# Attention steps every 14 groups, operand sums parked in memory, weight sums made one product earlier

## The chip, the cores and the metric

The kernel runs on one core of one Trainium2 chip. The metric is the device time of one execution in microseconds. A profile of one execution goes with it: TensorE (PE, with its weight loads PEld), VectorE (DVE), ScalarE (ACT), GpSimd (POOL, idle here) and SyncE (SP), on whose queue all transfers are issued.

## What is computed

One step of one decoder layer, for a new sequence of 1024 positions and eight sample streams of eight new tokens each, all in float32:

```
proj = einsum('bld,de->ble', x, w_in)          # 1088 rows, 2048 -> 10752
gb, gc, h, z_c, q, k, v, z_a, gate_c, gate_a = split(proj)
y_c = silu(z_c) * gb * short_conv(gc * h)
o   = window attention with sinks and ALiBi (prompt: blocks of 128; samples: 128 cached keys + 8 new)
y_a = silu(z_a) * o
merged = sigmoid(gate_c) * (y_c @ w_conv_out) + sigmoid(gate_a) * (y_a @ w_attn_out)
y = layer_norm(ALPHA * x + merged @ w_out)
```

The updated key and value windows and convolution states are returned too. For the sample streams, all but eight rows of each new window are the old cache, copied.

## The kernel before, in words

**Units and products.** Each large matrix product is cut into units: one unit makes 2 x 128 output columns for all 1088 rows over half of the inner dimension, by one level of the Strassen-Winograd scheme, with seven products instead of eight. Each product is four groups of six matmuls (each operand is split into a high and a low part of a reduced-precision type, and three of the four cross products are kept). A unit is thus 28 groups. Stage a does all 42 units (a0 to a41) with the first half of the inner dimension and stores the partial results (`pd<-ca`); stage b does them again with the second half (b0 to b41, in another order: keys and values, queries, gates, convolution), adding to what was stored (`cb<-pd`); stage m merges (m0_0 to m0_7 over the convolution's half, m1_0 to m1_7 over the attention's); a last stage multiplies by w_out and normalises. In the profile the accumulators of the units are `psa37a`, `psb0c`, `psm_0b` and so on. The three letters name three accumulators of one unit. Four of the seven products go into the first (a), so what a product left there has to be taken out (`take`, an addition into `ca`, `cb` or `cm`) before the product after the next one may start.

**Weights.** The weights of a unit (`wra`, `wrb`, `wrm`, 1 MB) are loaded during the unit before it. For products 2, 3 and 6 sums of weight blocks are needed, four DVE instructions per unit (into `wsa`/`wsb`/`wsm` or in place). Then ACT casts the high part and DVE subtracts to get the low part. `run` issues this three products ahead; the sums stand directly ahead of the cast that reads them, in `Unit.high`.

**Operands.** The other operand is the same for all units of a stage: seven sets of four tiles, resident in SBUF. When a stage's last unit ends, the next stage's set i replaces the old set i as soon as its product i is through (`Operands.put`): per tile a cast on ACT and a subtraction on DVE. Four of the seven sets are sums of loaded blocks, 16 DVE subtractions or additions in all: eight (`combine`) are made ahead, the eight for sets 4 and 5 (`t1` and `p4`) stand between the casts. `load_all` (called by `ahead_of`) issues 16 loads in one go.

**Attention and samples.** Everything else is put between the groups. `agenda` lists work by group number, and `tick` runs after each group: it does what is due, and one entry (`pieces`) of `line`, the operands' queue. An attention step is one head pair times one block of 128 rows, 64 steps in all, one every `STEP` groups, starting in unit b3; the table in `Step.__init__` says how many groups after the step's start each piece of it is issued. `sample` does the same for one of eight pieces of the sample attention, one per gate unit. All small accumulators (`sc`, `pt`, `po`, `sps`, `spo`) share two PSUM banks, `ax`, in turn: a third may only be written when all readers of the first are done.

**Order.** Every engine executes in the order in which the program issues (`InOrder` ties each instruction to the one before it on its engine), transfers on SP included. So one instruction that waits holds up everything behind it on its engine.

## Time and profile before

| | |
|---|---|
| time, median of 3 runs | 2726.74 us (2724.79 to 2728.77) |
| the profiled execution's own time | 2725.17 us |
| its span, first to last instruction | 2723.1 us |
| mean granted TensorE clock | 0.990 |
| PE busy | 2639.6 us, 97% of the span |
| DVE busy | 1757.8 us, 65% |
| ACT busy | 1057.7 us, 39% |
| transfers | 415.97 MB, 45.4% of 16 engines' span |

Busy time of PE is not peak rate: when the granted clock (PEclk) halves, matmuls take longer and count as busier. The length of a unit is therefore the plainer measure: a unit with no wait lasts 21.09 us (a36, a40, b23, b24 and all others of stage a but the first and a37), plus 1.3 us for each attention step within it and 2.1 us for a sample piece.

### The profile page before, as it was taken

What the parts mean: (1) busy time and instruction counts of PE and PEld (TensorE: products, weight loads), DVE (VectorE), ACT (ScalarE), POOL (GpSimd) and SP (SyncE); (2) the same over time, 40 slices, a digit from 0 to 9 for tenths busy, and PEclk for the clock granted to TensorE, in tenths of its full rate; (3) what the DMA queues carried; (4) which work ended last, traced back from release to release, by engine and by line L of the source; (5) the groups of instructions that cost most, each with busy time, mean ns of one, the idle gap of its engine ahead of it and who ended that gap; (6) DMA issues with size and microseconds to landing.
All of it is one profiled execution on the core that took longest, in us unless ns stands there. A gap on an engine that the chain in (4) does not pass through costs nothing. (4 is left out here: it accounts for less than half of the span.)

```text
span 2723.1 us, 47823 instructions
## 1 busy us (share of the span) xinstructions
PE 2639.6 (97%) x19426; PEld 2545.0 (93%) x19426; DVE 1757.8 (65%) x3371; ACT 1057.7 (39%) x2074; POOL 0.2 (0%) x4
## 2 busy tenths in 40 slices
PE   8999999999999999989989999999999999899998
PEld 7999999999999999989989999999999999788886
DVE  7444444444444878868878898888766867533836
ACT  4232332323222535555554545454432433322221
POOL 0000000000000000000000000000000000000000
PEclk9999999999999999999999999999999999999999
DMA  4322232223333366665545545455546565733543
GB/s 160 114 96 97 103 120 98 97 96 115 110 137 121 141 211 205 202 201 168 152 164 162 176 138 155 152 171 170 187 170 216 185 233 195 254 99 110 183 144 102
DMA packets 167327, 415.97 MB, mean 153 GB/s; under 512 B 23442, under 2 KB 75666, under 8 KB 139172
## 3 DMA queue, kind: packets, MB, share of 16 engines
q1 hardware_dynamic: 167108, 412.92, 45.4%
q8 instruction: 153, 2.51, 0.4%
q14 instruction: 66, 0.54, 0.1%
HBM read 295.33 MB, written 119.48 MB: 152 GB/s over the span
## 5 line engine op out<-in xcount | busy, mean ns | idle before, releaser
L97 PE MATMUL o<-wo,m 128*128 128x512 f32 x1344 | 320.6, 394 | 0.2 <-DVE r L1166 0.2
L97 PEld LDWEIGHTS o<-wo,m 128*128 128x128 f32 x1344 | 254.5, 189 | 55.7 <-issue 0.6
L97 DVE TENSOR_TENSOR wa<-wra,wa 128x512 fp32r<-128x512 f32 x210 | 144.5, 689 | 221.6 <-ACT wa L97 221.6
L97 ACT CAST wb<-wrb 128x512 fp32r<-128x512 f32 x210 | 127.3, 616 | 141.4 <-DVE wrb L97 129.3
L1088 DVE TENSOR_TENSOR wo<-wraw,wo 128x512 fp32r<-128x512 f32 x112 | 76.6, 686 | 148.9 <-ACT wo L1087 148.8
L97 DVE TENSOR_TENSOR wb<-wrb,wb 128x512 fp32r<-128x512 f32 x210 | 143.7, 684 | 42.1 <-ACT wb L97 40.4
L1087 ACT CAST wo<-wraw 128x512 fp32r<-128x512 f32 x112 | 69.3, 621 | 220.2 <-PE o L97 193.2
L97 ACT CAST wa<-wsa 128x512 fp32r<-128x512 f32 x84 | 52.1, 621 | 256.4 <-DVE wsa L97 256.4
L97 ACT CAST wa<-wra 128x512 fp32r<-128x512 f32 x210 | 126.3, 622 | 43.2 <-DVE wra L97 33.1
L97 DVE TENSOR_TENSOR wa<-wsa,wa 128x512 fp32r<-128x512 f32 x84 | 58.0, 692 | 93.2 <-ACT wa L97 93.1
L97 ACT CAST wb<-wsb 128x512 fp32r<-128x512 f32 x84 | 51.6, 614 | 152.6 <-DVE wsb L97 150.7
L97 ACT ACTIVATE p<-p,nm 128x256 f32<-128x256 f32 (+1 forms) x128 | 62.5, 489 | 88.7 <-DVE nm L97 88.5
L97 DVE TENSOR_TENSOR wm<-wrm,wm 128x512 fp32r<-128x512 f32 x80 | 55.1, 689 | 46.4 <-ACT wm L97 43.3
L97 ACT ACTIVATE p<-p,den 128x256 f32<-128x256 f32 (+1 forms) x128 | 56.5, 489 | 64.6 <-DVE den L97 63.1
L97 DVE TENSOR_TENSOR wb<-wsb,wb 128x512 fp32r<-128x512 f32 x84 | 57.7, 687 | 35.6 <-ACT wb L97 35.4
L97 ACT ACT_TABLE_LOAD x58 | 74.4, 1283 | 1.7 <-PEq L1331 0.7
L97 ACT CAST wm<-wsm 128x512 fp32r<-128x512 f32 x32 | 19.9, 621 | 107.9 <-DVE wsm L97 107.9
L97 ACT CAST wm<-wrm 128x512 fp32r<-128x512 f32 x80 | 48.4, 621 | 32.2 <-DVE wrm L97 30.5
L97 PEld LDWEIGHTS first<-xa,wa 128*128 128x128 f32 x336 | 46.7, 205 | 12.7 <-ACT wa L97 5.6
L97 PE MATMUL first<-xa,wa 128*128 128x272 f32 x336 | 48.1, 308 | 9.9 <-ACT wa L97 4.0
L97 DVE TENSOR_TENSOR o<-po,ot 64x128 f32<-64x128 f32 x128 | 35.9, 280 | 27.1 <-ACT ot L97 26.0
L97 DVE TENSOR_TENSOR pp<-pt,pp 128x512 fp32r<-128x512 f32 (+1 forms) x64 | 41.7, 651 | 12.9 <-ACT pp L97 12.8
(1072 smaller groups left out, 6507.3 us busy)
## 6 DMA issues: line engine op xcount, KB each, us to landing
pd<-ca SPq DMA_DIRECT2D x42, 1088.0 KB
cb<-pd SPq DMA_DIRECT2D x42, 1088.0 KB
wra<-in_win SPq DMA_DIRECT2D x42, 1024.0 KB
wrb<-in_win SPq DMA_DIRECT2D x42, 1024.0 KB
wraw<-in_wo SPq DMA_DIRECT2D x128, 256.0 KB
sgd<-cb SPq DMA_DIRECT2D x16, 1088.0 KB
sg<-sgd SPq DMA_DIRECT2D x64, 272.0 KB
qt<-qd SPq DMA_DIRECT2D x128, 128.0 KB
```

What stands on the lines that cost most here:

```text
L97: first = f(*args, **kw)
L1087: nc.scalar.copy(hi, raw)
L1088: nc.vector.tensor_sub(lo, raw, hi.bitcast(F32))
```

## The change

Six things change, and no matmul, DVE or ACT instruction is added or removed.

- `STEP` goes from 15 to 14 groups, so that a unit of 28 groups holds exactly two attention steps, and each step's pieces fall at the same places of every unit. The table of places is moved by up to two groups. The table of `sample` is stretched from 38 to 59 groups. The two sigmoids of a gate unit are now issued one directly after the other. One gate unit (`gate_unit(9)`) is moved ahead of the convolution's units, the two others between them are moved, and `open_merge` starts in `gate_unit(12)` instead of 13.
- The copies of the old caches (`copies`, two transfers of 960 KB within device memory) are issued at the start of unit a4 instead of with the samples, and the 16 small stores of new rows are spread, one every 5 groups.
- The weight sums get a function of their own (`Unit.sums`), issued at the end of each product for a product that is one further ahead than the cast.
- `Operands.begin` replaces `ahead_of` and `load_all` for x1 and for both halves of the merge: four loads every 7 or 8 groups; 44 or 50 groups after its start it makes all 16 sums, one after each group, and stores the sums for sets 4 and 5 (`t1`, `p4`) in device memory; it then loads two blocks again.
- `Operands.put` fetches `t1` and `p4` back instead of computing them.
- With this come 24 transfers more for each of the three operand sets, 72 in all.

```diff
-STEP = 15
+STEP = 14
...
+        def begin(self, gap, wait):
+            self.kept = {n: [dram(f"x{n}{self.name}{k}", [P, HALF]) for k in range(4)] for n in ("t1", "p4")}
...
+            for i, what in enumerate(((0, 1, "b"), (1, 1, "c"), (0, 0, "a"), (1, 0, "d"))):
+                after(1 + gap * i, lambda what=what: part(*what))
+            def sums():
+                t3, t2, t1, p4 = (parts[t] for t in "bacd")
+                for op, out, x, y in (
+                    (ve.tensor_sub, t3, t1, t3), (ve.tensor_add, t2, t3, t2),
+                    (ve.tensor_sub, t1, t1, t2), (ve.tensor_sub, p4, p4, t2),
+                ):
+                    for k in range(4):
+                        line.append(lambda op=op, out=out, x=x, y=y, k=k: op(out[k], x[k], y[k]))
+                    if out is t1:
+                        line.append(lambda: self.spill(t1, "t1"))
+                line.append(lambda: self.spill(p4, "p4"))
+                def rows():
+                    self.b11 = self.load(0, 0, "c")
+                    self.b21 = self.load(1, 0, "d")
+                line.append(rows)
...
             def again():
-                self.b22 = self.load(1, 1, "a")
+                if self.kept and i == 0:
+                    self.t1 = self.fetch("t1", "c")
+                if self.kept and i == 1:
+                    self.p4 = self.fetch("p4", "d")
+                if i == 2:
+                    self.b22 = self.load(1, 1, "a")
...
+        def make_sums(upto):
+            while summed[0] < min(upto, len(stream)):
+                u, i = stream[summed[0]]
+                u.sums(i)
+                summed[0] += 1
...
                 if k == 3:
                     for v, n in todo:
                         v.low(n)
+                    if g >= 14:
+                        make_sums(g + 2 + ahead(g))
...
-            begin={2: one_by_one, 37: lambda: ahead_of(x1)}.get(p),
+            begin={2: one_by_one, 4: copies, 37: lambda: x1.begin(8, 50)}.get(p),
...
-                (0, self.load), (14, self.scores), (16, self.biased), (17, self.maximum),
-                (19, self.exponents), (22, self.sums), (23, self.normed), (22, self.load_values),
-                (27, self.turn), (29, self.high), (30, self.low), (34, self.output),
-                (36, self.half), (37, self.joined), (38, self.gated),
+                (0, self.load), (14, self.scores), (16, self.biased), (18, self.maximum),
+                (20, self.exponents), (23, self.sums), (22, self.load_values), (24, self.normed),
+                (27, self.turn), (29, self.high), (31, self.low), (35, self.output),
+                (37, self.half), (39, self.joined), (40, self.gated),
...
-            (9, rows), (12, lambda: scores(0)), (15, lambda: scores(2)), (18, maximum), (20, exponents),
-            (24, sums_), (25, lambda: normed(0)), (26, lambda: normed(2)),
-            (27, lambda: turn(0)), (28, lambda: turn(1)), (29, lambda: turn(2)), (30, lambda: turn(3)),
-            (31, turn_new), (34, output), (36, heads), (38, gated),
+            (10, rows), (13, lambda: scores(0)), (27, lambda: scores(2)), (30, maximum), (32, exponents),
+            (36, sums_), (37, lambda: normed(0)), (38, lambda: normed(2)),
+            (39, lambda: turn(0)), (40, lambda: turn(1)), (41, lambda: turn(2)), (42, lambda: turn(3)),
+            (43, turn_new), (55, output), (57, heads), (59, gated),
...
-        ahead_of(xm[0])
+        xm[0].begin(7, 44)
...
-            if (b, i) == (0, 4):
-                u.begin = lambda: ahead_of(xm[1])
+            if (b, i) == (0, 3):
+                u.begin = lambda: xm[1].begin(8, 50)
```

**Place 1: DVE in unit b0**, while the operands of stage b are put in place. `cb<-cb,psb0..` are the takes, `xb<-..` the low parts of operands, `wb<-..` those of weights. Before:

```order
679 L97 TENSOR_TENSOR cb_9098<-cb_9098,psb0c 128x544
680 L97 TENSOR_TENSOR xdb_8062<-xdb_8062,xcb_8070 128x544
681 L97 TENSOR_TENSOR xb_0_9294<-xdb_8060,xb_0_9294 128x544
682 L97 TENSOR_TENSOR xdb_8064<-xdb_8064,xcb_8072 128x544
683 L97 TENSOR_TENSOR wb_5_9310<-wrb_8948,wb_5_9310 128x512
684 L97 TENSOR_TENSOR xb_1_9312<-xdb_8062,xb_1_9312 128x544
685 L97 TENSOR_TENSOR cb_9098<-cb_9098,psb0a 128x544
```

After:

```order
683 L97 TENSOR_TENSOR cb_9150<-cb_9150,psb0c 128x544
684 L97 TENSOR_TENSOR xb_1_9349<-xdb1p_9118,xb_1_9349 128x544
685 L97 TENSOR_TENSOR xb_2_9359<-xdb2p_9120,xb_2_9359 128x544
686 L97 TENSOR_TENSOR xb_3_9370<-xdb3p_9122,xb_3_9370 128x544
687 L97 TENSOR_TENSOR wb_5_9368<-wrb_8990,wb_5_9368 128x512
688 L97 TENSOR_TENSOR wrb_8990<-wrb_8990,wsb_9204 128x512
689 L97 TENSOR_TENSOR cb_9150<-cb_9150,psb0a 128x544
```

The subtractions `xdb<-xdb,xcb` are gone from between the takes (as are the four `xbb<-xab,xcb` ahead of them), the low parts read the fetched tiles `xdb0p` to `xdb3p`, and the weight sum `wrb<-wrb,wsb` has moved up by one product.

**Place 2: SP at the start of unit a4.** `pd<-ca` stores a unit's result, `wra<-in_win` loads the next unit's weights. After (before, the two rows in the middle aren't there):

```order
28 L97 DMA wra_1004<-in_win 128x2048
29 L97 DMA pd_66<-ca_911 128x2176
30 L97 DMA out_k_s<-in_ck 8x2x15360
31 L97 DMA out_v_s<-in_cv 8x2x15360
32 L97 DMA wra_1214<-in_win 128x2048
```

The weights of unit a5 now stand behind the two copies.

**Place 3: DVE from product 5 of unit b23 to product 1 of unit b24**, where the 16 sums for the merge are now made (`xam`, `xbm`, `xcm`, `xdm` are the loaded blocks). After, the last 12 rows up to the first take of b24:

```order
2336 L97 TENSOR_TENSOR xcm_21485<-xcm_21485,xam_21543 128x544
2337 L97 TENSOR_TENSOR xcm_21487<-xcm_21487,xam_21545 128x544
2338 L97 TENSOR_TENSOR xcm_21489<-xcm_21489,xam_21547 128x544
2339 L97 TENSOR_TENSOR wb_2_21859<-wsb_21841,wb_2_21859 128x512
2340 L97 TENSOR_TENSOR wrb_21680<-wrb_21680 128x512
2341 L97 TENSOR_TENSOR cb_21577<-cb_21577,psb23a 128x544
2342 L97 TENSOR_TENSOR xdm_21601<-xdm_21601,xam_21541 128x544
2343 L97 TENSOR_TENSOR xdm_21603<-xdm_21603,xam_21543 128x544
2344 L97 TENSOR_TENSOR xdm_21605<-xdm_21605,xam_21545 128x544
2345 L97 TENSOR_TENSOR wb_3_21898<-wrb_21680,wb_3_21898 128x512
2346 L97 TENSOR_TENSOR xdm_21607<-xdm_21607,xam_21547 128x544
2347 L97 TENSOR_TENSOR cb_21799<-cb_21799,psb24a 128x544
```

Seven of these twelve rows are sums for the merge; the program before has none of them between these takes.

**Place 4: DVE at the turn of two sample units**, from the last take of b12 to the first of b13. `st`, `tn`, `sqs`, `skt`, `spa` belong to the sample attention, `p`, `pp`, `nm` to an attention step. After, with the four pairs `st`/`tn` left out but for the last:

```order
1160 L97 TENSOR_TENSOR cb_12760<-cb_12760,psb12a 128x544
...
1168 L97 TENSOR_SCALAR st_1_12784<-st_1_12784,sden_1_12789 32x128
1169 L97 TENSOR_SCALAR tn<-st_1_12784,sden_1_12789 32x8
1170 L97 COPY skt_0_13150<-qkvs 64x4x8
1171 L97 COPY sqs_0_13154<-qkvs 64x4x8 x4
1172 L97 TENSOR_TENSOR pp_1_13284<-pt_1_13249,pp_1_13284 128x512
1173 L97 STREAM_TRANSPOSE spa_1_12785<-st_1_12784 32x128
1174 L97 TENSOR_TENSOR wb_3_13296<-wrb_12943,wb_3_13296 128x512
1175 L97 TENSOR_REDUCE nm_2_13330<-p_2_13298 128x2
1178 L97 STREAM_TRANSPOSE spa_1_12785<-st_1_12784 32x128
1179 L97 TENSOR_TENSOR cb_13126<-cb_13126,psb13a 128x544
```

With the new tables this sequence stands at the same place of every sample unit; before, it fell elsewhere in each.

## Prediction

> **What bounds the kernel now.** First the page's busy line:

> ```profile
> span 2723.1 us, 47823 instructions
> PE 2639.6 (97%) x19426; PEld 2545.0 (93%) x19426; DVE 1757.8 (65%) x3371; ACT 1057.7 (39%) x2074; POOL 0.2 (0%) x4
> ```

> PE is the bound. The change takes no matmul away, so it can only give back time in which PE stands still or runs at a low clock. Where that is, the windows show, cut at the borders of units (length, busy time of PE, PEld, DVE, ACT, POOL, granted clock, DMA share, GB/s):

> ```profile
> core 0: us, PE busy (x) PEld busy (x) DVE busy (x) ACT busy (x) POOL busy (x), PEclk, DMA share, GB/s
> 780.84:801.93 21.09, 21.09 (x170) 21.09 (x169) 9.32 (x14) 6.28 (x11) 0.00 (x0) 1.00 0.30 104
> 801.93:830.18 28.25, 23.48 (x170) 23.26 (x169) 10.44 (x16) 6.38 (x11) 0.00 (x0) 0.88 0.64 235
> 914.65:941.83 27.18, 22.04 (x170) 21.28 (x169) 25.52 (x42) 12.19 (x21) 0.00 (x0) 1.00 0.48 171
> 1126.75:1420.18 293.43, 269.00 (x2048) 256.13 (x2047) 227.15 (x622) 168.54 (x399) 0.00 (x0) 0.97 0.56 173
> 1217.71:1243.81 26.10, 26.10 (x209) 24.98 (x208) 22.36 (x67) 15.48 (x38) 0.00 (x0) 1.00 0.43 137
> 1420.18:1901.51 481.33, 476.75 (x3787) 471.41 (x3786) 409.16 (x905) 240.97 (x514) 0.00 (x0) 1.00 0.49 159
> 1965.37:1992.39 27.02, 22.15 (x170) 21.27 (x169) 25.44 (x40) 14.50 (x24) 0.00 (x0) 1.00 0.28 88
> 2140.70:2169.45 28.75, 23.69 (x171) 22.80 (x170) 27.60 (x44) 13.15 (x23) 0.00 (x0) 0.94 0.58 189
> ```

> The rows are a36 (a clean unit, 21.09), a37, b0, the ten units b9 to b18, one of them alone (b12), the next twenty, m0_0 and m1_0. PE's waits name the causes (total, times, longest):

> ```profile
> engine line waited for: us in total, times, longest us
> PE po L97 <- DMA vt<-vcd: 9.0, 1, 9.0
> PE psm_0a L97 <- ACT cm L97: 7.4, 4, 3.1
> PE psa37a L97 <- DVE ca L97: 4.8, 1, 4.8
> PE psb1a L97 <- DVE cb L97: 1.2, 1, 1.2
> ```

> An attention step's own price is needed to tell work from waiting. Its three pieces on PE:

> ```profile
> 1259.43 0.60 PE L97 MATMUL pt<-ident,p 128*128 128x128 f32 x4
> 1259.78 1.75 PE L97 MATMUL psb13a<-xb,wb 128*128 128x272 f32 x12
> 1261.37 0.65 PE L97 MATMUL sc<-kt,qt 128*128 128x256 f32 x4
> 1261.86 1.67 PE L97 MATMUL psb13a<-xb,wb 128*128 128x272 f32 x12
> 1265.63 0.64 PE L97 MATMUL po<-pp,vt 128*128 128x256 f32 x4
> 1266.10 0.92 PE L97 MATMUL psb13b<-xb,wb 128*128 128x272 f32 x6
> ```

> From start to next start 0.35 + 0.49 + 0.47 = 1.31 us. In b12 PE is never idle, so 26.10 is work alone: 21.09, two steps 2.62, and 2.4 left for a sample piece.

> **The change part by part.** Over-lengths against 21.09 plus this work are what can be won.

> *Operands for stage b (unit a37).*

> ```profile
> 815.15 0.33 SPq L97 DMA_DIRECT2D wra<-in_win  x1
> 822.92 1.14 ACT L97 CAST wa<-wra 128x512 fp32r<-128x512 f32 x2 [8.12 <-DMA wra<-in_win]
> 824.95 5.40 PE L97 MATMUL psa37a<-xa,wa 128*128 128x272 f32 x24 [4.77 <-DVE ca L97]
> ```

> The 16 operand loads stand ahead of the weights on SP, so these are issued at 815.15. Their cast waits, the take queued behind it on DVE waits, and so does PE, 4.77, and then 24 matmuls last 5.40 instead of 3.18. With four loads every 8 groups there are at most four ahead of the weights. I take the whole 28.25 - 21.09 = **-7.2**. The 16 sums of x1 fall into a38 and a39, where DVE has 21.09 - 9.32 = 11.8 us free against 16 x 0.63 = 10.1 (spacing below): nothing.

> *Put in b0, m0_0 and m1_0.*

> ```profile
> L97 DVE TENSOR_TENSOR xdb<-xdb,xcb 128x544 f32<-128x544 f32 x4 | 2.9, 720 | 0.0
> L97 DVE TENSOR_TENSOR xbb<-xab,xcb 128x544 f32<-128x544 f32 x4 | 2.9, 718 | 0.0
> 929.59 0.72 DVE L97 TENSOR_TENSOR cb<-cb,psb0a 128x544 f32<-128x544 f32 x1
> 930.22 0.72 DVE L97 TENSOR_TENSOR xdb<-xdb,xcb 128x544 f32<-128x544 f32 x1
> ```

> DVE is busy 25.52 us in b0, more than a clean unit lasts: it is the bound there. Eight subtractions of 0.72 leave; 25.52 - 5.8 = 19.7 fits under 21.09. So b0 loses 27.18 - 21.09 = 6.1, less 0.5 that I leave for a late take: **-5.6**. In b1 the late take (1.2) stands behind the same queue, of which I take **-0.9**. m0_0: 25.44 - 5.8 = 19.6, so 5.9 less 0.5, **-5.4**. m1_0: 27.60 - 5.8 = 21.8 is still 0.7 over the clean unit; of 28.75 - 21.09 = 7.7 I take **-6.5**. Cover: the fetched tiles (1.1 MB a set) have two to four products of 3.01 us to land.

> *Attention and samples.* b9 to b18: ten units 210.9, eight sample pieces 19.2, 18.7 steps (280 groups by 15) 24.5, together 254.6, so 38.8 of 293.43 are over. The twenty units behind: 421.8 + 35 x 1.31 = 467.7, so 13.6 over. Together 52.4. A part of it hangs on SP:

> ```profile
> 1182.31 7.63 SPq L97 DMA_DIRECT2D out_v_s<-vn  x8
> 1189.98 0.72 SPq L97 DMA_DIRECT2D out_v_s<-in_cv  x1
> 1191.76 0.37 SPq L97 DMA_DIRECT2D vt<-vcd  x1
> ```

> `vt`, behind both cache copies, two loads and 16 small stores, costs PE the 9.0; copies and stores leave this place, so 9.0 goes, and with it the slow matmuls that follow such a stop (in a37 28.25 - 21.09 - 4.77 = 2.4). The others are small accumulators whose bank still has a reader:

> ```profile
> 1382.09 0.43 PE L97 MATMUL spo<-spn,vn 32*64 32x128 f32 x2 [2.62 <-DVE pp L97]
> 1383.29 3.02 PE L97 MATMUL psb17a<-xb,wb 128*128 128x272 f32 x12
> 1396.44 1.08 PE L97 MATMUL sps<-skt,sqs 64*32 64x136 f32 x4 [3.62 <-DVE o L97]
> ```

> With 15 groups against 28 such meetings fall elsewhere in each unit; with 14 they are the same in all. By the new order the small products of a sample unit come in the groups 0 (`sc`), 5 (`sps`), 7 (`po`), 13 (`pt`), 14 (`sc`), 19 (`spo`, `sps`), 21 (`po`) and 27 (`pt`), two banks in turn: each has the readers of the last but one to wait for, five groups or more, 3.8 us, behind it but for the `po` in 21. Only at the turn of two sample units (Place 4) do DVE's rows between two takes fill the two products of 3.01 us and the pieces in them. I leave 1.0 for each of eight sample units, the size of the wait in b1, and 6.5, half of what the twenty show, for the rest: 52.4 - 14.5 = **-37.9**.

> *Cache copies in a4.* They go ahead of the weights of a5 on SP.

> ```profile
> 107.10 0.38 SPq L97 DMA_DIRECT2D wra<-in_win  x1
> 118.62 1.14 ACT L97 CAST wa<-wra 128x512 fp32r<-128x512 f32 x2
> 123.94 3.18 PE L97 MATMUL psa4a<-xa,wa 128*128 128x272 f32 x24
> 1182.50:1189.00 6.50, 6.50 (x50) 5.75 (x50) 2.55 (x8) 6.37 (x11) 0.00 (x0) 1.00 0.43 159
> ```

> After the first copy SP stood for 7.63, and the engines were 43% busy. Two such are 15 us. Weights would land at 107.1 + 15 + about 3 = 125, while the cast may come 2.0 before product 6 (822.92 against 824.95), at 121.9. Late 3; then some slow matmuls: **+3.5**. Bounds: 0, if the transfers run side by side, since less than half of the engines were busy; 10, if both follow each other as in a37, where an issue 9.8 us before PE's go was already 4.8 late. The middle is nearest to the row of 7.63.
> [...]

> *Sums for the merge in b23 and b24.* Place 3: from the start of product 4 of b23 (12.05 into the unit) DVE has 28 rows to the first take of b24, at 0.63 (929.59 to 930.22) 17.8 us: 29.9. Product 2 of b24 is due at 21.09 + 6.03 = 27.1. Late 2.8; then full or half clock:

> ```profile
> 1974.41 3.28 PE L97 MATMUL psm_0a<-xm,wm 128*128 128x272 f32 x24 [2.85 <-ACT cm L97]
> ```

> After 2.62 idle 12 matmuls took 3.02 instead of 1.75; after 2.85 idle 24 took 3.28, hardly more than 3.18. Between 0 and a37's 2.4 for the slow spell I take half: **+4.0** (0, if DVE works ahead, to 5.2). The sums for m1 fall beside a lighter queue in m0_4 and m0_5: **+0.5**.
> [...]

> *At nothing:* weight sums one product earlier and the two sigmoids side by side add no instruction; should the earlier sums push a take back, that costs what the takes of the twenty units wait now, the 6.5 I left there; the spread stores lie on an SP that has gaps; 72 more transfers of some 20 MB meet DMA shares of 0.28 to 0.64 in those units.

> **Sum:** -7.2 - 5.6 - 0.9 - 5.4 - 6.5 - 37.9 + 3.5 + 4.0 + 0.5 = -55.5. The profiled execution took 2725.2; 2669.7 by this. The median is 1.6 above it: **2671 us**.

> **The rivals.** *The waits stay and move.* Fixed places make a fixed gap, not a wider one: DVE has as many rows as before in these units (227 us in 293). Then only the 9.0 with its slow clock (11.4) and a third of the rest goes (13.7), 25 instead of 37.9, and the copies cost 7: sum -38, up to -20; about 2690 to 2706. For it: the mean wait in the twenty units is small and spread over takes that no table moves. Against: the largest waits after the 9.0, 3.62 and 2.62, are meetings.

> *Everything is hidden.* Copies run beside the weights, b24's take comes in time, 4 remain of 52.4: -3.5 - 4.0 - 10.5 more, 2653.

> *A collision at a fixed place (the slower side).* What happened once by chance, 2.62 and 3.62 with the 2.4 of slow matmuls, returns in every unit that holds the same pieces. It takes 55.5 / 8 = 6.9 in each sample unit, or 55.5 / 32 = 1.7 in each unit with two steps, to cancel all that is won; 2.0 in the 32 adds 64, and 2735 comes out. For it: the `po` in group 21 stands two groups, 1.5 us, behind the `spo` whose bank it takes, and the copies that read `spo` stand on ACT behind two exponentials that need a maximum from DVE. Against: a DVE that is late there costs PE what it is late, about 1 us as in b1, and mostly in the eight sample units alone, and every other reader has 3.8 us.

> *The change doesn't reach PE.* If a37's weights are still late because its loads are only spread, and b0's fetches wait, 25 of the gain go and 2697 is left; only with the second case together it is no change.

> **How the numbers follow.** Forecast (2655 to 2688) 0.64; waits that move (2688 to 2706) 0.16; everything hidden (2645 to 2655) 0.10; transfers late (around 2697) 0.03; collision 0.07, of which 0.02 within 0.2%. A measurement of this kernel can tell 0.2%, 5.5 us, from no change. Faster 0.93, same 0.02, slower 0.05. The range is 2650 to 2704: below, 17 us for attention's rest, copies and sums all at their good ends; above, copies at 10, sums at 5, attention at two thirds, put at half in two places.

> **What would show it.** Right: a37, b0, m0_0 under 22 us; no `vt` wait; the units with two steps about 23.7 to 24, those with samples about 27; a4 some 3.5 and b24 some 4 longer than their work. Wrong: a wait that returns at the same place in many units; `wra` late in a37 again; `xb` or `xm` waiting on a DMA in b0 or m0_0; a4 as short as 21.1.

## The result and the profile after

The changed kernel takes 2665.36 us (median of 4 runs, 2663.21 to 2668.40) against 2725.76 of the kernel before on the same chip (4 runs): a ratio of 0.978, 95% interval 0.9763 to 0.9797. 2671 was predicted, with 2650 to 2704 as the range. The profiled execution took 2665.85, its span 2664.1, so 59.0 less than before.

The page's head, after:

```profile
span 2664.1 us, 48073 instructions
PE 2617.3 (98%) x19426; PEld 2532.4 (95%) x19426; DVE 1748.7 (66%) x3371; ACT 1046.6 (39%) x2068; POOL 0.2 (0%) x4
```

PE's 22 us less of busy time is in part matmuls that no longer run at a lower clock: b9 to b18 had a granted clock of 0.97, and now have 1.00. But 7.7 of it are in the twenty units behind, whose granted clock is 1.00 before and after; what those are was not taken apart. The rest of the 59.0 is waiting. The six fewer ACT instructions are table loads (52 instead of 58); four of them go with the two sigmoids that now stand side by side (in the old order, shown below, 54 with them and 58 without). The units after, cut at their borders as in the prediction (a37; a4; b0; b9 to b18; the next twenty units; b24; m0_0; m1_0):

```profile
core 0: us, PE busy (x) PEld busy (x) DVE busy (x) ACT busy (x) POOL busy (x), PEclk, DMA share, GB/s
804.49:825.58 21.09, 21.09 (x170) 21.09 (x169) 9.24 (x14) 6.19 (x11) 0.00 (x0) 1.00 0.86 315
106.42:129.50 23.08, 21.36 (x170) 21.14 (x169) 8.33 (x13) 6.29 (x11) 0.00 (x0) 1.00 0.49 180
909.95:933.64 23.69, 21.81 (x170) 21.24 (x169) 21.58 (x36) 11.41 (x21) 0.00 (x0) 1.00 0.57 204
1118.39:1377.07 258.68, 258.47 (x2054) 249.79 (x2053) 225.28 (x619) 165.01 (x399) 0.00 (x0) 1.00 0.61 192
1377.07:1846.09 469.02, 469.02 (x3772) 468.01 (x3771) 406.50 (x899) 233.38 (x500) 0.00 (x0) 1.00 0.50 170
1867.18:1890.76 23.58, 21.34 (x171) 21.15 (x170) 17.91 (x29) 7.17 (x12) 0.00 (x0) 1.00 0.93 337
1911.85:1934.85 23.00, 21.62 (x170) 21.18 (x169) 20.16 (x32) 13.60 (x23) 0.00 (x0) 1.00 0.44 151
2083.93:2107.72 23.79, 21.64 (x171) 21.19 (x169) 22.94 (x36) 13.02 (x25) 0.00 (x0) 1.00 0.74 242
```

The striking rows are the fourth and fifth: in thirty units of attention PE is idle for 0.2 us. PE's longest waits after, outside the first and the last stage (one more, `psm_0b` on ACT's `cm`, is 1.3 in two):

```profile
PE psm_0a L97 <- ACT cm L97: 2.3, 2, 1.2
PE psb24a L97 <- DVE cb L97: 2.2, 1, 2.2
PE psa4a L97 <- DVE ca L97: 1.7, 1, 1.7
PE psb0a L97 <- ACT wb L97: 1.1, 1, 1.1
```

Term by term (length after minus length before, us):

| place | predicted | measured |
|---|---|---|
| a37 | -7.2 | -7.2 |
| b0 | -5.6 | -3.5 |
| b1 | -0.9 | -0.7 |
| attention and samples (b9 to b18 and the next twenty) | -37.9 | -47.1 (-34.8 and -12.3) |
| m0_0 | -5.4 | -4.0 |
| m1_0 | -6.5 | -5.0 |
| a4 | +3.5 | +2.0 |
| b24 | +4.0 | +2.5 |
| m0_5 and m0_6 | +0.5 | +1.4 |
| first stage, b2, b25, m0_7, last stage | 0 | +2.6 |
| sum | -55.5 | -59.0 |

So the sum was near, and its largest term was 9 too small while three others were 5 too large. That these errors cancel is luck. What the experiments had to settle is which of the edits made the 47.1, since the prediction gave it to the fixed places and to the cache copies, and nothing to the earlier weight sums.

### The profile page after: what moved, and what is told of

It reads as the page before. It is cut to its first block, busy times and chain, and to the rows that moved or that the text cites. A ratio compares the mean times of both kernels' runs of the same rounds, so it can differ in the third digit from the quotient of the medians.

```text
span 2664.1 us, 48073 instructions
## 1 busy us (share of the span) xinstructions
PE 2617.3 (98%) x19426; PEld 2532.4 (95%) x19426; DVE 1748.7 (66%) x3371; ACT 1046.6 (39%) x2068; POOL 0.2 (0%) x4
## 5 line engine op out<-in xcount | busy, mean ns | idle before, releaser
L97 DVE TENSOR_TENSOR wa<-wra,wa 128x512 fp32r<-128x512 f32 x210 | 144.6, 689 | 271.8 <-ACT wa L97 271.8
L97 PE MATMUL o<-wo,m 128*128 128x512 f32 x1344 | 320.5, 393 | 0.2 <-DVE r L1230 0.2
L97 PEld LDWEIGHTS o<-wo,m 128*128 128x128 f32 x1344 | 254.8, 190 | 56.0 <-issue 0.6
L97 ACT CAST wb<-wrb 128x512 fp32r<-128x512 f32 x210 | 129.3, 618 | 109.9 <-DVE wrb L97 89.2
L97 DVE TENSOR_TENSOR wb<-wrb,wb 128x512 fp32r<-128x512 f32 x210 | 143.8, 685 | 1.1
L97 ACT CAST wa<-wra 128x512 fp32r<-128x512 f32 x210 | 126.5, 622 | 19.3 <-DVE wra L97 12.0
L97 ACT CAST wa<-wsa 128x512 fp32r<-128x512 f32 x84 | 52.3, 622 | 165.1 <-DVE wsa L97 165.1
L97 DVE TENSOR_TENSOR wa<-wsa,wa 128x512 fp32r<-128x512 f32 x84 | 57.8, 689 | 87.4 <-ACT wa L97 87.1
L97 ACT ACTIVATE p<-p,nm 128x256 f32<-128x256 f32 (+1 forms) x128 | 62.5, 489 | 97.5 <-DVE nm L97 97.3
L97 DVE TENSOR_TENSOR wm<-wrm,wm 128x512 fp32r<-128x512 f32 x80 | 55.1, 688 | 38.7 <-ACT wm L97 38.4
L97 ACT ACTIVATE p<-p,den 128x256 f32<-128x256 f32 (+1 forms) x128 | 56.5, 489 | 47.6 <-DVE den L97 45.2
L97 ACT CAST wb<-wsb 128x512 fp32r<-128x512 f32 x84 | 51.4, 612 | 58.4 <-DVE wsb L97 58.4
L97 ACT CAST pp<-pt 128x512 fp32r<-128x512 f32 (+1 forms) x64 | 35.9, 561 | 65.8 <-PE pt L97 65.1
L97 ACT CAST wm<-wrm 128x512 fp32r<-128x512 f32 x80 | 48.3, 621 | 31.4 <-DVE wrm L97 31.4
L97 PEld LDWEIGHTS first<-xa,wa 128*128 128x128 f32 x336 | 46.6, 205 | 13.4 <-ACT wa L97 5.9
L97 DVE TENSOR_TENSOR wb<-wsb,wb 128x512 fp32r<-128x512 f32 x84 | 57.5, 684 | 2.5 <-ACT wb L97 1.7
L97 PE MATMUL first<-xa,wa 128*128 128x272 f32 x336 | 48.0, 307 | 10.6 <-ACT wa L97 4.4
L97 DVE TENSOR_TENSOR cm<-cm,sg 128x544 f32<-128x544 f32 x64 | 46.3, 724 | 9.1 <-DMA sg<-sgd 4.0
L97 ACT CAST wm<-wsm 128x512 fp32r<-128x512 f32 x32 | 19.9, 621 | 78.9 <-DVE wsm L97 78.9
```

Of the source, the lines that this page charges most:

```text
L97: first = f(*args, **kw)
```

## The experiments

Effects of a few us are read from the lengths of units in the profiles. Many of these repeat closely: b3 to b8 last 139.3 to 139.6 in every kernel here. In the following, "attention" is b9 to b18 and the twenty units behind, as above; it lasts 727.7 to 727.8 in the changed kernel and in four of the others. Not every unit repeats so well: b0 lasts between 22.8 and 23.7 in five kernels that have it alike, and b24 lasts 23.6 in three and 25.1 in a fourth.

**The old places back.** The changed kernel with the old numbers where pieces are issued (steps and samples), and the old order of the gate units:

```
-STEP = 14
+STEP = 15
-  (18, self.maximum), (20, self.exponents), (23, self.sums), ...
+  (17, self.maximum), (19, self.exponents), (22, self.sums), ...
...
-    gate_unit(12, open_merge)
-    gate_unit(13)
+    gate_unit(13, open_merge)
```

> The changed kernel with the places of the attention steps, of the sample pieces and of the gate units as they were before (a step every 15 groups, both old tables, the old order of the gate units); copies, spread stores, weight sums and operands stay as changed. Theory 'fixed places': of the 47.1 us that attention and samples gained, about 36 hang on the places (47.1 less the 9.0 of the vt wait and 2.4 of slow matmuls behind it): 36 of them come back, 2701 us, and waits of sps, sc and spo on DVE of 2 to 4 us are seen again. Rival 'SP and early sums did it': under 10 come back, 2665 to 2675.

2693.87 us, ratio to before 0.9896 (0.988 to 0.9913). Attention, two windows as above:

```profile
1118.07:1392.18 274.11, 264.91 (x2049) 253.59 (x2048) 225.58 (x619) 162.10 (x392) 0.00 (x0) 0.98 0.57 177
1392.18:1865.55 473.37, 471.50 (x3787) 470.62 (x3785) 410.38 (x906) 242.28 (x516) 0.00 (x0) 1.00 0.49 162
```

274.11 - 258.68 and 473.37 - 469.02 are 15.4 and 4.4: 19.8 come back, with waits of `sps` and `spo` on `pp` (3.1 and 2.5 in all). A wait of 7.1 in b25 is no part of it: in this order the merge's operands start one unit later, and b25 is 11.2 longer for it. Neither theory fits: the places, taken out of the changed kernel alone, are worth 20 of the 47, not 36 and not under 10.

**The weight sums late again.** Only the call that makes them a product earlier is taken out:

```
                     for v, n in todo:
                         v.low(n)
-                    if g >= 14:
-                        make_sums(g + 2 + ahead(g))
```

> The changed kernel with the weight sums made directly ahead of their cast again, as before; all else as changed. With the old places back, 19.8 of the 47.1 us that attention and samples had gained came back, and b11's 12 us for the load of vt did not, so some 15 us are unexplained. Theory 'the early sums give the takes room': b3 to b18 and the twenty units behind get waits of PE on DVE takes (psb.. on cb) or on casts again, +10 to +15 there. Rival 'early sums do nothing by themselves': within 3 us of the changed kernel there.

2693.64 us, ratio 0.989 (0.9861 to 0.9918): as much as all places together. Attention, then m0_0 and m1_0:

```profile
1119.98:1384.36 264.38, 259.49 (x2054) 249.90 (x2053) 226.04 (x619) 165.53 (x399) 0.00 (x0) 1.00 0.59 188
1384.36:1862.52 478.16, 473.95 (x3773) 468.85 (x3771) 407.01 (x900) 233.04 (x499) 0.00 (x0) 1.00 0.49 166
1931.23:1958.91 27.68, 23.84 (x170) 23.62 (x169) 22.05 (x34) 14.58 (x25) 0.00 (x0) 0.88 0.46 164
2110.58:2136.85 26.27, 22.86 (x170) 22.64 (x169) 24.05 (x39) 13.19 (x24) 0.00 (x0) 0.94 0.70 230
```

Attention loses 5.7 + 9.1 = 14.8, as much as the theory expected, but not where it expected it. PE's waits there, but for one of 0.6 for a take:

```profile
PE sps L97 <- DVE sqs L97: 4.8, 7, 0.8
PE pt L97 <- ACT p L97: 3.1, 5, 0.6
```

The first comes once in each of b12 to b18, 4.4 to 4.8 us into the unit: the small form of a wait that returns at a fixed place. The waits add up to 8.5; where the rest of the 14.8 lies was not found out. What the theory did not expect at all is m0_0: 27.68, no shorter than the 27.02 before, though its operand sums are still fetched and DVE is busy for 22.05 of it only. Why, the rows of this kernel show (DVE, ACT and PE in m0_0):

```profile
1935.02 0.72 DVE L97 TENSOR_TENSOR cb<-cb,psb25a 128x544 f32<-128x544 f32 x1
1935.65 0.69 DVE L97 TENSOR_TENSOR wrm<-wrm 128x512 f32<-128x512 f32 x1
1936.44 0.62 ACT L97 CAST wm<-wrm 128x512 fp32r<-128x512 f32 x1 [2.16 <-DVE wrm L97]
1936.97 2.10 ACT L97 ACTIVATE cb<-cb 128x1088 f32<-128x1088 f32 x2
1940.61 0.60 ACT L97 COPY cm<-psm_0a 128x544 f32<-128x544 f32 x1
1941.26 4.00 PE L97 MATMUL psm_0a<-xm,wm 128*128 128x272 f32 x16 [3.84 <-ACT cm L97]
```

The sum `wrm` stands behind a take on DVE, the cast of it waits on ACT, and behind the cast stand the sigmoids, four casts and the take `cm`, for which PE waits 3.84 and then runs 16 matmuls in 4.00. In the changed kernel the same sum stands ahead of the take:

```profile
1913.47 0.69 DVE L97 TENSOR_TENSOR wrm<-wrm 128x512 f32<-128x512 f32 x1
1914.07 0.72 DVE L97 TENSOR_TENSOR cb<-cb,psb25a 128x544 f32<-128x544 f32 x1
1914.27 0.62 ACT L97 CAST wm<-wrm 128x512 fp32r<-128x512 f32 x1 [2.66 <-DVE wrm L97]
1918.44 0.60 ACT L97 COPY cm<-psm_0a 128x544 f32<-128x544 f32 x1
1919.10 3.28 PE L97 MATMUL psm_0a<-xm,wm 128*128 128x272 f32 x24 [1.06 <-ACT cm L97]
```

No instruction more or less, 1.06 instead of 3.84. Between cast and `cm` lie 4.2 us in both; what differs is how long after the start of the unit the cast can begin, 5.2 (1936.44 - 1931.23) or 2.4 (1914.27 - 1911.85).

**Both back, and the sigmoids too.** The two edits above together, and then with the sigmoids apart as before:

```
-        after(2, lambda: sigmoid(1))
-        after(2, lambda: sigmoid(0))
+        after(1, lambda: sigmoid(0))
+        after(4, lambda: sigmoid(1))
```

> The old places and the late weight sums together; copies, spread stores and operands as changed. If the two are independent, the loss against the changed kernel in b9 to b18 and the twenty units is 19.8 plus what the run with late sums alone loses. Theory 'they work together' (a place is only safe if the takes are in time): it is clearly more, 30 to 35, and only the 12 of the vt wait remain won. Rival 'independent': the sum of both within 3 us.

> As places_and_sums_back, and the two sigmoids of a gate unit apart again (one and four groups after the unit, as before). That run lost 55.6 us in b9 to b18 and the twenty units against the changed kernel, 8.5 more than the kernel before loses there, though it has no long wait for vt. Theory 'two sigmoids in one go hold up ACT for 3.5 us, which hurts where places and sums have no room': the loss falls by 15 to 22, to 34 to 40 us, and the time to about 2722. Rival 'sigmoids don't matter, old places and late sums together are worse with spread stores': it stays within 4 us of 55.6 and 2741.7.

With places and sums back: 2741.74 us, ratio 1.0073 (1.005 to 1.0096), slower than the kernel before. With the sigmoids apart too: 2719.73, ratio 0.9987 (0.9976 to 0.9998). Attention in the first and in the second:

```profile
1121.35:1420.25 298.90, 272.29 (x2048) 258.68 (x2047) 227.11 (x622) 163.12 (x394) 0.00 (x0) 0.96 0.52 163
1420.25:1904.69 484.44, 477.72 (x3787) 471.36 (x3786) 409.02 (x905) 241.86 (x514) 0.00 (x0) 1.00 0.48 158
```

```profile
1118.51:1401.53 283.02, 266.90 (x2048) 253.65 (x2047) 226.93 (x622) 168.55 (x399) 0.00 (x0) 0.98 0.55 173
1401.53:1882.87 481.34, 476.70 (x3787) 471.38 (x3785) 409.06 (x905) 241.01 (x514) 0.00 (x0) 1.00 0.49 159
```

The first lost 55.6 against the changed kernel, more than the 47.1 that were to be lost. With the sigmoids apart it is 36.7, so in this order 19.0 came from two sigmoids in one go. They hold ACT for 2.1 us at a stretch. With them PE's waits in attention grow: `sps` on `pp` from 1.5 to 7.3, `sps` on `o` from 2.5 to 5.0, `pt` on `p` from 2.6 to 5.6. That the sigmoids hold up the casts and exponentials behind them is argued from this, not shown.

Places and sums were each taken out alone only with the sigmoids in one go: 19.8 and 14.8. In that same state both together cost 55.6, which is 21.0 more than the sum, so there they do work together. With the sigmoids apart both cost 36.7, near 34.6; that they are independent then is not shown, as neither was tried alone there. The 10.4 by which b9 to b18 are then still shorter than before fit the burst on SP, whose two halves, each mended in the kernel before (below), shorten b9 to b18 by 10.5 and 7.8. Along this one path the 47.1 are **20 places, 15 early sums, 10 the burst on SP, 2 left over**; with the steps in another order the shares would be others. What the paired sigmoids do in the new order by themselves was not tried.

**The early sums in the kernel before.** The same edit, the other way round:

```
+                    if g >= 14:
+                        make_sums(g + 2 + ahead(g))
```

> The kernel before with one thing changed: the weight sums made one product further ahead than their cast, as in the changed kernel. In the changed kernel taking this away alone cost 28 us. Theory 'the early sums are worth that much by themselves, because a take no longer stands behind a sum and the cast that reads it': b9 to b18 and the twenty units gain about 20 already here (places_and_sums_back against places_back says 25 and 11), m0_0 and m1_0 some 2 each: 2695 to 2705. Rival 'they only work with fixed places and parked sums': under 8 us, 2715 to 2725.

2707.69 us, ratio 0.9939 (0.9924 to 0.9954): 15 us won by this edit alone, of which b9 to b18 make 8.4 and the twenty units 7.8; m0_0 stays at 26.8, m1_0 gains 1.1 and b0 1.6. Between the two theories: the part in attention comes in both kernels (16.2 here, 14.8 there), most of the part in m0_0 and m1_0 only together with the fetched operand sums.

**What held `vt` up.** Two kernels, each the kernel before with one part: the copies in a4, or the small stores one every 5 groups:

```
-            begin={2: one_by_one, 37: lambda: ahead_of(x1)}.get(p),
+            begin={2: one_by_one, 4: copies, 37: lambda: ahead_of(x1)}.get(p),
...
-                dq.dma_start(dst[:, : WIN - ST, :], old[:, ST:, :])
```

```
         after(10, store)
+        for i, (src, dst) in enumerate(((kn, k_s), (vn, v_s))):
+            for b in range(NS):
+                after(12 + 5 * (8 * i + b), lambda src=src, dst=dst, b=b: store_new(src, dst, b))
```

> The kernel before with one thing changed: the two cache copies at the start of unit a4. Theory 'the copies hold vt up': b11 goes from 38.3 to about 27, a4 from 21.1 to 23.1, -9 in all. Rival 'the burst of 16 small stores holds SP': b11 stays above 33.

> The kernel before with one thing changed: the 16 small stores of new rows are issued one every 5 groups, the cache copies stay where they were. Theory 'the copies hold vt up': b11 stays above 35. Rival 'the burst of small stores does': b11 falls to about 27, -11 in all.

2717.99 and 2717.22, both 0.998 (0.9968 to 0.9991). b11, 38.28 long before, with the copies moved, and then with the stores spread, where a wait for `vt` is left:

```profile
1180.23:1208.90 28.67, 27.04 (x209) 25.08 (x208) 22.11 (x64) 17.19 (x38) 0.00 (x0) 1.00 0.56 174
```

```profile
1177.86:1208.01 30.15, 28.21 (x209) 26.56 (x207) 22.82 (x65) 18.56 (x43) 0.00 (x0) 0.94 0.68 227
```

```profile
PE po L97 <- DMA vt<-vcd: 1.9, 1, 1.9
```

Either edit alone takes most of it (b11 is 9.6 and 8.1 shorter). So it was mainly the two in a row that cost the 9.0: eight small stores took SP 7.63 behind a copy, and take 2.6 with no copy ahead. So in the changed kernel the copies could stay where they were:

```
-            begin={2: one_by_one, 4: copies, 37: ...}
+            begin={2: one_by_one, 37: ...}
         after(10, store)
+        after(11, copies)
```

> The changed kernel with the two cache copies back among the samples (one group after the last rows of keys and values are stored), all else as changed. Theory 'the copies hold up vt': unit a4 returns to 21.09 (-2.0) and a wait of PE for a load of 5 to 9 us comes back near b11, in all +3 to +9. Rival 'the small stores held up SP, and they are spread now': no wait for a load comes back, only the -2.0 shows.

2667.00 us. a4 is 21.10 again (-2.0), b11 is 27.16 instead of 25.33 (+1.8), and PE waits for no load; the 1.8 is mostly one wait of 1.6, of `po` for `den` on DVE. Moving the copies to a4 was worth nothing once the stores are spread.

**The operand sums computed again.** In the changed kernel `t1` and `p4` are made in the put, not fetched:

```
-                if k < 4 and i in (4, 5) and not self.kept:
+                if k < 4 and i in (4, 5):
                     line.append(lambda k=k: (t1, p4)[i - 4](k))
```

> The changed kernel with the eight sums t1 and p4 of each later operand set computed during the put again, not fetched (the early sums are then 8 and not 16, and the stores and fetches are gone). Theory 'DVE is what holds the put': b0 goes back by about 3.5 to 27, m0_0 by 4 to 27, m1_0 by 5 to 28.7, while b24 with half as many early sums loses most of its 2.5 and m0_5 its 1.1: in all about +9. Rival 'the order of the casts holds it': b0, m0_0 and m1_0 stay within 1 us of 23.7, 23.0 and 23.8.

2670.48 us. b0, m0_0 and m1_0 (b24 is 21.09 again):

```profile
909.80:935.24 25.44, 22.58 (x171) 21.37 (x170) 25.33 (x43) 11.88 (x20) 0.00 (x0) 1.00 0.51 183
1911.33:1937.13 25.80, 22.48 (x170) 21.36 (x169) 24.77 (x40) 14.51 (x24) 0.00 (x0) 1.00 0.37 128
2084.79:2113.26 28.47, 22.48 (x170) 21.35 (x169) 28.18 (x45) 13.91 (x25) 0.00 (x0) 1.00 0.53 179
```

DVE is again busy for nearly the whole of these units, and they are 1.7, 2.8 and 4.7 longer than in the changed kernel (b0 by up to 2.7, as it varies by 0.9); b24 loses its 2.5 and m0_5 and m0_6 their 1.4. So the fetched sums won 9.2 and cost 3.9, which is 5.3 where about 9 was expected.

**A meeting built on purpose.** Twice the sample table was moved so that the copies that read `spo` are issued after the attention's `po`, the second time with the second half of the scores a group later as well, so that its bank too has a reader behind:

```
-  (27, lambda: scores(2)), (30, maximum), ...  (55, output), (57, heads), (59, gated),
+  (27, lambda: scores(2)), (30, maximum), ...  (56, output), (60, heads), (62, gated),
...
-  (27, lambda: scores(2)), (30, maximum), ...  (55, output), (57, heads), (59, gated),
+  (28, lambda: scores(2)), (31, maximum), ...  (55, output), (60, heads), (62, gated),
```

> The changed kernel with three entries of the sample table moved: the output product one group later, directly ahead of the attention's output product, its copies on ACT three groups later than now. This builds the meeting that the rival on the slower side spoke of: the attention's po takes the bank of spo, whose readers come after it. Theory 'a meeting at a fixed place repeats': each of the eight sample units gets a wait of po on ACT of 2 to 3 us, +16 to +25 in all. Rival 'the other bank is free by then': no wait, within 3 us of the changed kernel.

> The changed kernel with the second half of the sample scores one group later (just behind the output product of the samples) and the copies that read that output three groups later: when the attention's po comes, both banks still have readers that are issued after it. Theory 'a meeting at a fixed place repeats in every unit': a wait of po of 1 to 2 us in each of the eight sample units, b11 to b18 +8 to +16. Rival 'one bank comes free in time all the same': within 2 us of the changed kernel there.

2667.14 and 2664.07 us; b9 to b18 last 258.79 and 258.81, where the changed kernel has 258.68. The theory missed both times. The first does not test it: there `sps` comes at 1236.49, `spo` at 1238.02 and `po` at 1239.82, so two banks used in turn give `po` the bank of `sps`. In the second, where `spo` comes ahead of `sps`, b13 shows why:

```profile
1236.24 0.65 PE L97 MATMUL sps<-skt,sqs 64*32 64x136 f32 x4
1236.98 0.48 DVE L97 TENSOR_TENSOR st<-sps,sbias 32x136 f32<-32x136 f32 x2
1237.67 0.64 PE L97 MATMUL po<-pp,vt 128*128 128x256 f32 x4
1239.60 0.76 ACT L97 COPY so<-spo 64x32 f32<-64x32 f32 x4
```

`po` starts two us ahead of the copies that read `spo`, so it did not take that bank: it took the one of `sps`, free when `st` is done. So the two banks are not used strictly in turn, as the description of the kernel has it; it looks as if whichever is free first is given out. A meeting needs late readers of both, and I did not build one that costs anything. What it would cost stays open.

**The new costs mended.** The copies four groups later, behind the load of a5's weights, and the first merge sums nine groups earlier:

```
-            begin={2: one_by_one, 4: copies, 37: ...}
+            begin={2: one_by_one, 4: lambda: after(4, copies), 37: ...}
-        xm[0].begin(7, 44)
+        xm[0].begin(7, 35)
```

> The changed kernel with the three new costs mended: the cache copies four groups later, behind the load of a5's weights; the 16 sums for the merge's first operands nine groups earlier (35 groups after the start, so that they end within b23), those for the second six groups earlier. Theory: a4 -2.0, b24 -2.5, m0_5 and m0_6 -1.4, together -5.9: 2659.5 us. Rival: the sums at their new place run into other takes, or wait for their loads, and the copies delay the store or the load of the next unit: no gain, 2663 to 2668.

(The sums of the second set were not moved in the kernel that ran, so the 1.4 of m0_5 and m0_6 could not go.) 2661.13 us, ratio 0.9771 (0.9755 to 0.9787). a4, and b23 and b24:

```profile
107.15:128.24 21.09, 21.09 (x171) 21.09 (x169) 9.24 (x14) 6.19 (x11) 0.00 (x0) 1.00 0.50 197
1845.03:1866.50 21.47, 21.45 (x170) 21.18 (x169) 19.13 (x31) 4.86 (x7) 0.00 (x0) 1.00 0.53 201
1866.50:1887.60 21.10, 21.10 (x171) 21.10 (x169) 14.21 (x22) 7.45 (x12) 0.00 (x0) 1.00 0.86 314
```

a4 and b24 are clean units; b23 and m0_6 got 0.4 longer each (m0_6 varies by as much, 21.4 to 21.9, in kernels that have it alike). By the units it is 3.7 faster than the changed kernel, where 5.9 was expected; by the times alone (intervals 0.9763 to 0.9797 and 0.9755 to 0.9787) the two can't be told apart.

## Why the prediction was right, and where it was not

*a37 and the stall behind its loads: right to 0.1 us.* The weights are in time although the DMA engines are busier than before (share 0.86 instead of 0.64), because only four loads stand ahead of them.

*Attention: right in direction, its size and its reasons off.* The prediction left 14.5 us, 1.0 for each sample unit because DVE's rows fill the time between two takes, and half of the waits of the twenty units. Nothing is left. The step that failed is "At nothing: weight sums one product earlier": without them the changed kernel loses 14.8 in attention, 4.7 in m0_0 and 2.5 in m1_0, that is the whole gain of m0_0 and half of that of m1_0, which the prediction gave to the fetched operand sums alone. I had looked at what the edit adds, which is nothing, and not at what stands behind a sum in its queue. The share that I gave to the places (26 of 37.9, the rest being the 11.4 of `vt`) was measured at 20.

*The wait for `vt`: right that it goes, half right why.* Copies and small stores in a row did it; either edit would have won most of it, and moving the copies bought nothing on top.

*Put in b0, m0_0, m1_0: right mechanism, 5.0 too large.* The run with computed sums shows that DVE was the bound. But DVE's busy time fell by 3.9, 5.3 and 4.7, not by the 5.8 that I subtracted, so that in b0 (21.58) and by more than forecast in m1_0 (22.94) it still does not fit under 21.09. And I took the whole over-length as DVE's, less 0.5 to 1.2. The waits that are left end with another queue: ACT, whose casts and takes stand behind one another (`psm_0a` on `cm` 2.3, `psm_0b` on `cm` 1.3, `psb0a` on `wb` 1.1).

*a4: +2.0 for +3.5, with a wrong step.* I read the 7.63 as SP held by a copy, twice, hence 15 us. After the change SP isn't held at all:

```profile
107.63 0.86 SPq L97 DMA_DIRECT2D out_k_s<-in_ck  x1
108.54 1.34 SPq L97 DMA_DIRECT2D out_v_s<-in_cv  x1
109.99 0.51 SPq L97 DMA_DIRECT2D wra<-in_win  x1
...
124.35 1.14 ACT L97 CAST wa<-wra 128x512 fp32r<-128x512 f32 x2 [5.07 <-DMA wra<-in_win]
...
126.38 3.28 PE L97 MATMUL psa4a<-xa,wa 128*128 128x272 f32 x24 [1.72 <-DVE ca L97]
```

The load is issued at 109.99, and half of it lands only when the copies are through. The packets of the trace, by size and burst, show it (bytes, number, first start, last end):

```
61440 x 8   111.23  114.16      out_k_s and out_v_s: four rounds of 8 packets
61440 x 8   113.85  116.83
61440 x 8   116.69  119.10
61440 x 8   118.96  121.36
 8192 x 64  112.27  117.41      wra: one half
 8192 x 64  121.23  123.82      wra: the other half
```

Each round is 8 packets side by side, 2.3 to 2.9 us each, and a copy takes two rounds, 5.1 us. Half of the weights pass beside them by 117.4, the other half comes when the copies are through: the two copies took 10.1 us, and the half of the load behind them another 2.5. So neither of my two bounds held: one half of the load ran side by side with the copies, the other followed them.

*b24: +2.5 for +4.0.* The stall is 2.24 (2.8 forecast by counting rows), and no slow matmuls followed it: 24 in 3.25. That was the coin that I had put at half, and it fell the lucky way: in the first of the two kernels with the moved sample table the same stop, 2.23, is followed by 24 matmuls in 4.68, and b24 is 4.0 longer, as forecast (the last section shows where the two stops fell). The cause is the one named: with the sums nine groups earlier the unit is clean.

*Second set of sums: +1.4 for +0.5*, m0_5 waits 0.8 for a take on ACT, not on DVE.

*The rivals.* "The waits stay and move" fell: nothing stayed. "Everything is hidden" is nearest to what happened in the attention units, but for a4 and b24. "A collision at a fixed place" did not occur in the changed kernel, and the second attempt to make it occur shows that its premise, two banks strictly in turn, was wrong. That a wait can return at one place in unit after unit the run with late sums shows, at 0.4 to 0.8 us each. "The change doesn't reach PE" fell with a37. (The parts of the first rival add up to -39, not -38.)

*The last stage*, 405.6 instead of 402.95, was not foreseen. In the profiles of all the kernels here it lasts between 402.5 and 406.2 although none of them touches it, with waits of `o` on DVE that come and go. It is not explained by the change; what decides it was not tried.

## What to carry to other kernels

An instruction moved earlier in a queue can be worth a lot (15 us for the weight sums in the kernel before) or cost something (2.5 for the merge's sums in b24): ask what stands behind it, on its own engine and on the engine that reads it, and whether a wait there ends later than it must. Where two periodic patterns share a queue, make one period divide the other, and then place the pieces; and where several edits are made at once, take each out alone and two together, the small ones too: here a side edit, the paired sigmoids, cost 19.0 in one order of the rest, and places and sums looked as if they alone worked together. In a4 half of a load issued behind two copies came in beside them by 117.4, and the other half only behind them, by 123.8, so issue the urgent one first: four groups of delay for the copies were enough (a4 back at 21.09).

## What the runs showed of the hardware that was not expected

A stop of PE didn't always lower the clock behind it, and its length alone didn't decide. Without slow matmuls: 1.72 (a4, 24 matmuls in 3.28), 2.24 (b24, 24 in 3.25), 2.85 before (24 in 3.28). With them: 2.62 before (12 in 3.02), 3.84 with late sums (16 in 4.00), 4.77 before (24 in 5.40), and 2.23 in the same place of b24 in the first kernel with the moved sample table (24 in 4.68). In the traces of the kernel before and of the changed kernel the granted clock is at half, between 60 us and the last 15, for 3.41, 6.83 or 10.24 us at a time, and these changes lie whole multiples of 3.41 us apart. Two neighbouring stretches of that length around the stop of 2.23, with the granted clock behind the busy times:

```profile
1875.25:1878.66 3.41, 1.36 (x11) 1.39 (x12) 3.41 (x7) 1.27 (x3) 0.00 (x0) 1.00 0.99 415
1878.66:1882.08 3.42, 3.42 (x18) 3.42 (x17) 0.99 (x3) 0.63 (x2) 0.00 (x0) 0.50 1.00 364
```

PE is idle for 2.05 of 3.41 us, and the next stretch has half the clock. In the changed kernel, cut in the same way, the stop of 2.24 falls on two stretches, 1.13 and 1.11 idle, and the clock stays at 1.00:

```profile
1871.09:1874.50 3.41, 2.28 (x19) 2.06 (x17) 3.41 (x6) 3.33 (x5) 0.00 (x0) 1.00 1.03 349
1874.50:1877.91 3.41, 2.30 (x18) 2.33 (x19) 3.40 (x6) 0.33 (x1) 0.00 (x0) 1.00 0.98 400
1877.91:1881.33 3.42, 3.42 (x29) 3.42 (x28) 1.32 (x2) 1.24 (x2) 0.00 (x0) 1.00 0.97 333
```
